# Seven-product matrix sums: the second sum of a unit begun from a copy of the first product, and x normalised by even and odd tokens

## The chip, the core and the metric

The kernel runs on one core of a Trainium2 chip. Each core has a matmul engine (TensorE, PE in the profile, with its weight loads as PEld), VectorE (DVE), ScalarE (ACT), GpSimd (POOL) and SyncE (SP), which run side by side and wait for each other by semaphores. Matrices lie in SBUF, matmul results in PSUM, which has eight banks of 128 x 512 float32. The metric is device time in microseconds of one execution. Before the change it is 1780.31 us, the median of three runs (1779.6 to 1780.34).

## What is computed

A decoder of two layers on 512 tokens of width 1024, all float32. In each layer, cut to what matters here:

```python
x = x + 0.5 * swiglu(rms_norm(x, ffn1_norm[l]), ffn1_w_in[l], ffn1_w_out[l])
h = rms_norm(x, mix_norm[l]) @ w_mix_in[l]
y = concatenate([short_conv_mixer(...), hgrn2_mixer(...), fox_mixer(...)])
x = x + y @ w_mix_out[l]
x = x + 0.5 * swiglu(rms_norm(x, ffn2_norm[l]), ffn2_w_in[l], ffn2_w_out[l])

def swiglu(h, w_in, w_out):
    gate, up = split(h @ w_in, 2)      # w_in is 1024 x 5632, w_out 2816 x 1024
    return (silu(gate) * up) @ w_out
```

The two layers have four of these SwiGLU blocks. The change touches nothing else; the three token mixers stay as they are.

## The kernel before

**Tiling.** x is held transposed in `xT` (128 features x 8 blocks x 512 tokens). A float32 factor is split in a rounded part `hi` (float32r) and the remainder `lo`, and `mm3` (L423) makes each product of blocks from three matmuls: hi x hi (L429), hi x lo (L435), lo x hi (L436). ScalarE makes hi, VectorE makes lo.

**A SwiGLU block.** The 22 blocks of 128 hidden features are taken in pairs. `cover` (L668) does the first 6 (first SwiGLU) or 4 (the others) in the plain way, while the norm of x is found; its table `ENTRY` says at which step the norm, the normalised quarters of x, their splitting and other small work are put in. Then `halved` (L823) does the rest by a scheme of seven products in place of eight for a 2 x 2 block product. A pair of hidden blocks is a unit of the way in, ("I", w): the two halves are of the 1024 features, of gate and up, and of the tokens. The hidden blocks are cut in three chunks (`CHUNKS`); while chunk c + 1 goes in, chunk c goes out to x, in two units ("O", (c, g)), g being one of two column groups. The last chunk goes out plainly (the matmuls with hh).

**The order.** `plan` (L90) writes it out: patterns such as "IIIIO" + "IIO" * 11 + "IOIO" interleave the products of both ways. The first SwiGLU has 84 such products, the others 91, and each is 24 matmuls of 256 columns. Per product n, `plan` also lists smaller work: loads of a 512 x 256 quarter of the weights into one of eight buffers x0 to x7 (SyncE, L854), a transfer that adds a second quarter onto it (GpSimd, L858 and L901), sums of quarters on VectorE (`total`, L871: S2 is the sum S of two quarters, S3 the difference of S and a third), sums of hidden values (L898) and the splitting of hidden values for a way-out product (`moving`, L887). Work that may move is put where `load`, an estimate of VectorE's work per product, is least.

**One product.** The loop that begins at L955 takes product n, then:

- `prepare` (L873) for product n + 3: ScalarE rounds its weights (L883), and after the product's own work VectorE takes the remainder (L885). There are three buffers hl, so this begins when product n has ended;
- for a way-in unit: P1 goes to a bank `a`, and ScalarE copies its negative to SBUF as g1 (L978); P2 has a bank of its own, VectorE takes g1 - P2 (L981), ScalarE the Silu of it (L324). P6 is accumulated on P1 in bank a, and ScalarE copies it to g2 (L985); P5 goes to a third bank and is copied to u2 (L988); P7 goes on in bank a and VectorE adds it to u2 (L991); P3 goes on in P5's bank and is added to g2 (L994), then Silu; after P4, VectorE multiplies out the hidden values (L1008, L1009 in the last chunk, which ScalarE and VectorE then split to hh, L1018 and L1019);
- for a way-out unit: VectorE adds the product, halved and with its sign, to the quarters of x that need it (L973), once for each of the seven.

ScalarE, VectorE, GpSimd and SyncE take this work each in one fixed order (`follow`), so an instruction that waits holds up all behind it on its engine.

**Normalising.** `normalise` (L787) multiplies a quarter of x (four feature blocks x 256 tokens) by gain and inverse norm, in four instructions (L793), stored token after token. `two` (L810) splits a quarter or a sum of quarters (L719) to hi and lo (L816, L817, L821) and reads it by a step of two: all even tokens, then all odd ones, which is how the matmul takes them.

**Banks.** `bank` takes the next of a tag's banks (mm 3, sc 2, pt 2, po 1) from a pool that rotates. A SwiGLU's way in uses one set of four (mm and po, or sc and pt), its way out the other.

Of the kernel before, what the change touches and what calls it, by code (L numbers as in the profile page):

```python
# [8 lines left out]
F32 = mybir.dt.float32  # L9
# [5 lines left out]
ALU = mybir.AluOpType  # L15
# [62 lines left out]


def plan(covered):  # L80

# [21 lines left out]
    def between(a, b, *what):  # L103
# [51 lines left out]
    for c in range(2):  # L155
        n0 = {p: at["O", (c, 0), p] for p in ORDER_OUT}

        last = at["I", CHUNKS[c + 1][0] + (4, 2)[c], "P4"] - 1

        place = {}  # L160
        for i, p in enumerate(ORDER_OUT):
            a = at["O", (c, 1), ORDER_OUT[i - 2]] if i > 1 else n0["P2"] - 3
# [36 lines left out]
class Trunk:  # L199
# [8 lines left out]
    def __init__(self, ctx, tc):  # L208
        self.tc = tc
        self.nc = tc.nc  # L210
        nc = self.nc
        self.uid = 0
        self.ntog = 0
        self.tab, self.tab_users = None, []
# [92 lines left out]

    def bank(self, tag):
        return self.ps.tile([P, T], F32, tag=tag, name=self.n(tag), bufs=BANKS[tag])

# [357 lines left out]
    def cover(self, fp, w_in, w_out, covered, mean, begin):  # L668
# [28 lines left out]
        def squares():  # L697

            norm.append(self.bank("pt" if self.ntog % 2 == 0 else "po"))
            i = self.sum_norm(norm[0])  # L700
            if begin is None:
                self.follow("p", i)
# [84 lines left out]
    def normalise(self, fp, a, b):  # L787

        H = T // 2
        t = fp.tile([P, 4, H], F32, tag=f"r{2 + 2 * a + b}", name=self.n("xn"))  # L790
        for k in range(4):
            i = 4 * a + k
            self.follow("v", self.nc.vector.scalar_tensor_tensor(  # L793
                out=t[:, k, :], in0=self.xT[:, i, b * H : (b + 1) * H],
                scalar=(self.gain if a == b else self.ngain)[:, i : i + 1],
                in1=self.inv[:, b * H : (b + 1) * H], op0=ALU.mult, op1=ALU.mult,
            ))
        self.xn[a, b] = t
# [11 lines left out]
    def two(self, hi, lo, src, other):  # L810

        nc = self.nc
        src = src.rearrange("p k t -> p (k t)").rearrange("p (n h) -> p h n", h=2)
        if other:
# [8 lines left out]
    def halved(self, fp, w_in, w_out, covered, deal):  # L823
# [63 lines left out]
        def moving(c, p):  # L887

            hi, lo = (
                fp.tile([P, 2, T], F32R, tag=f"m{w}", name=self.n("m"), bufs=2) for w in "hl"  # L890
            )
            a, v = self.two(hi, lo, self.quarter(fp, c, *SUM[p]), p in NEGATIVE)
            A(a), V(v)
            mov[c, p] = hi, lo
# [32 lines left out]
        self.hh, self.hl = [], []  # L927
        names = (("mm", "mm", "mm", "po"), ("sc", "sc", "pt", "pt"))

# [13 lines left out]
        ring = {"I": (self.ntog + 1) % 2, "O": self.ntog % 2}  # L943
        used = {"I": 0, "O": 0}
# [10 lines left out]
        for n, (kind, w, p) in enumerate(seq):  # L955
            u = kind, w
            new = ("P1", "P2", "P5")
            k = {"P2": "c", "P5": "b", "P3": "b"}.get(p, "a")
            if p in new:
                work[u, k] = bank(kind)  # L960
            acc = work[u, k]
            product(u, p, acc, p in new, p in ("P2", "P3", "P4"), n in (0, 7))
            rest = prepare(*seq[n + LEAD]) if n + LEAD < len(seq) else None
            if kind == "O":
                c, g = w

                for r, b, f in {
                    "P2": ((0, 0, -0.5),), "P1": ((0, 0, -0.5),), "P5": ((1, 1, -0.5),),
                    "P6": ((0, 1, -0.5),), "P7": ((1, 1, 0.5),), "P3": ((0, 1, 0.5),),
# [6 lines left out]
            elif p == "P1":  # L976
                work[u, "g1"] = g1 = tmp("g1")
                A(nc.scalar.activation(g1, acc, AF.Copy, scale=-1.0))  # L978
            elif p == "P2":
                g1 = work[u, "g1"]  # L980
                V(nc.vector.tensor_sub(g1, g1, acc))  # L981
                A(self.act(g1, g1, AF.Silu))
            elif p == "P6":
# [904 lines left out]
```

## Time and profile before

| | |
|---|---|
| median of the runs | 1780.31 us (1779.6 to 1780.34) |
| the profiled execution | 1781.39 us, its span in the profile 1779.6 us |
| granted TensorE clock | 1.000 |
| PE busy in the span | 1761.0 us, 99% |
| DVE busy | 1439.3 us, 81% |
| ACT busy | 1022.1 us, 57% |
| POOL busy | 176.9 us, 10% |
| seven-product stretches (us from the span's start) | 77.6 to 304.3, 615.6 to 863, 936 to 1183.3, 1494 to 1741.5 |
| mean transfer rate | 147 GB/s |

How to read it: an instruction stands as line, engine, operation, out<-in by the program's names, shape and number. A group's idle time is what its engine sat idle just before its instructions, and the arrow names what ended it. TensorE's matmuls are pipelined: each is shown from its start to a modelled end, which overlaps the next ones, so a busy TensorE says less than the distance between the starts. A lost stretch of TensorE's time is found where two starts lie further apart than usual.

### The profile page before, as it was taken

The numbers are of one execution on the slowest core, as the hardware profiler recorded it, in microseconds if no ns is written. First come the engines' busy times: TensorE is split into PE (matmuls) and PEld (weight loads), VectorE is DVE, ScalarE is ACT, GpSimd is POOL, SyncE is SP. The second block draws the span as 40 slices with busy tenths as digits, with TensorE's granted clock in tenths as the row PEclk, the third lists the DMA queues.
The fourth block names the chain that finished last, engine by engine and source line by source line (L and its number), as shares of the span: only waits on it lengthen the run. The fifth ranks groups of instructions, "written<-read, shape, count | busy, mean of one in ns | idle before, by whom it ended". The sixth has DMA issues, their size and how long they took to land.

```text
span 1779.6 us, 33419 instructions
## 1 busy us (share of the span) xinstructions
PE 1761.0 (99%) x13613; PEld 1644.1 (92%) x13613; DVE 1439.3 (81%) x1991; ACT 1022.1 (57%) x1417; POOL 176.9 (10%) x174
## 2 busy tenths in 40 slices
PE   9999999999999999999999999999999999999999
PEld 7999999888888899999989999998878888999998
DVE  7989888678687888889689897876777779888883
ACT  5555555465666565555456555555656656555652
POOL 0011120100000101112001111201000001020210
PEclk9999999999999999999999999999999999999999
DMA  7659784243543867869276787823434438687762
GB/s 213 189 126 195 182 177 105 75 117 89 134 108 103 237 137 164 194 167 177 83 210 138 172 186 198 168 73 83 119 92 128 122 102 218 167 159 198 157 141 95
DMA packets 257466, 262.35 MB, mean 147 GB/s; under 512 B 25832, under 2 KB 236528, under 8 KB 257312
## 3 DMA queue, kind: packets, MB, share of 16 engines
q1 hardware_dynamic: 201456, 192.02, 36.0%
q0 software_dynamic: 55840, 68.19, 24.0%
q8 instruction: 107, 1.75, 0.4%
q14 instruction: 47, 0.39, 0.1%
q10 hardware_dynamic: 16, 0.00, 0.0%
HBM read 226.15 MB, written 2.17 MB: 128 GB/s over the span
## 4 chain that ended last, share of the span: by engine, by line
PE 81%; DVE 10%; ACT 5%; issue 2%; DMA 2%; SPq 0%; ACTq 0%; DVEq 0%
PE mm L429 11%; PE mm L436 11%; PE mm L435 11%; PE pt L435 5%; PE pt L436 5%; PE pt L429 5%; PE sc L436 5%; PE sc L429 5%; PE sc L435 5%; PE po L429 3%; PE po L435 3%; PE po L436 3%; DVE hl L416 2%; DVE hl L885 2%; ACT hl L413 1%
## 5 line engine op out<-in xcount | busy, mean ns | idle before, releaser
L883 ACT CAST hl<-w 128x1024 fp32r<-128x1024 f32 x322 | 337.3, 1049 | 305.3 <-PE mm L436 71.6
L885 DVE TENSOR_TENSOR hl<-w,hl 128x1024 fp32r<-128x1024 f32 x322 | 393.3, 1223 | 61.2 <-ACT hl L883 61.1
L416 DVE TENSOR_TENSOR hl<-st,hl 128x1024 fp32r<-128x1024 f32 (+3 forms) x152 | 160.1, 1054 | 108.9 <-ACT hl L413 107.9
L413 ACT CAST hl<-st 128x1024 fp32r<-128x1024 f32 (+3 forms) x151 | 137.6, 911 | 162.9 <-PE po L436 77.2
L429 PE MATMUL mm<-xc,hl 128*128 128x256 f32 (+1 forms) x730 | 200.7, 275 | 1.2 <-ACT g L985 0.8
L436 PE MATMUL mm<-xc,hl 128*128 128x256 f32 x728 | 200.4, 275 | 0.6 <-DVE hl L885 0.6
L435 PE MATMUL mm<-xc,hl 128*128 128x256 f32 x728 | 200.3, 275 | 0.0
L429 PE MATMUL sc<-xc,hl 128*128 128x256 f32 (+1 forms) x530 | 145.9, 276 | 2.9 <-ACT g L985 2.3
L436 PE MATMUL sc<-xc,hl 128*128 128x256 f32 x528 | 145.4, 275 | 0.6 <-DVE hl L885 0.6
L435 PE MATMUL sc<-xc,hl 128*128 128x256 f32 x528 | 145.3, 275 | 0.0
L429 PEld LDWEIGHTS mm<-xc,hl 128*128 128x128 f32 x730 | 140.1, 192 | 2.0 <-ACT g L985 0.9
L436 PEld LDWEIGHTS mm<-xc,hl 128*128 128x128 f32 x728 | 139.8, 192 | 0.9 <-DVE hl L885 0.9
L435 PEld LDWEIGHTS mm<-xc,hl 128*128 128x128 f32 x728 | 139.8, 192 | 0.0
L429 PE MATMUL pt<-xc,hl 128*128 128x256 f32 (+1 forms) x482 | 132.1, 275 | 0.0
L435 PE MATMUL pt<-xc,hl 128*128 128x256 f32 x480 | 132.1, 275 | 0.0
L436 PE MATMUL pt<-xc,hl 128*128 128x256 f32 x480 | 132.0, 275 | 0.0
L429 PE MATMUL mm<-x,hl 128*128 128x512 f32 x272 | 105.8, 389 | 0.0
L429 PEld LDWEIGHTS sc<-xc,hl 128*128 128x128 f32 x530 | 101.7, 192 | 4.1 <-ACT g L985 2.7
L435 PE MATMUL mm<-x,hl 128*128 128x512 f32 x272 | 103.1, 379 | 0.0
L436 PE MATMUL mm<-x,hl 128*128 128x512 f32 x272 | 103.1, 379 | 0.0
L436 PEld LDWEIGHTS sc<-xc,hl 128*128 128x128 f32 x528 | 101.4, 192 | 0.9 <-DVE hl L885 0.9
L435 PEld LDWEIGHTS sc<-xc,hl 128*128 128x128 f32 x528 | 101.4, 192 | 0.0
(506 smaller groups left out, 5471.0 us busy)
## 6 DMA issues: line engine op xcount, KB each, us to landing
w<-in_ffn_w_in_dram SPq DMA_DIRECT2D x140, 512.0 KB, 5.9
w<-in_ffn_w_out_dram SPq DMA_DIRECT2D x64, 512.0 KB, 5.2
w<-in_ffn_w_out_dram POOLq DMA_DIRECT2D x56, 512.0 KB, 8.6
w<-in_ffn_w_in_dram POOLq DMA_DIRECT2D x39, 512.0 KB, 8.4
st<-in_w_mix_in_dram SPq DMA_DIRECT2D x72, 256.0 KB, 3.0
st<-in_ffn_w_in_dram SPq DMA_DIRECT2D x70, 256.0 KB, 3.8
w<-S POOLq DMA_DIRECT2D x35, 512.0 KB, 4.8
st<-in_ffn_w_out_dram SPq DMA_DIRECT2D x24, 512.0 KB, 3.6
```

The source lines that it names most:

```text
L413: a = nc.scalar.copy(hi, src[:, c : c + w])
L416: b = nc.vector.tensor_sub(lo, src[:, c : c + w], hi)
L429: i = nc.tensor.matmul(acc[:, c], ah, bh[:, c.start // 2 : c.stop // 2, :], start=first and c.start == 0, stop=False, skip_group_check=True,)
L435: nc.tensor.matmul(acc, ah, bl, start=False, stop=False, skip_group_check=True)
L436: i = nc.tensor.matmul(acc, al, bh, start=False, stop=last, skip_group_check=True)
L883: A(nc.scalar.copy(hi, src))
L885: return lambda: V(nc.vector.tensor_sub(lo, src, hi))
```

## The change

It has four parts.

1. Units for which `seeded` is true (all four way-out units, and the way-in units 10, 12, 14, 18 and 20, between whose P1 and P2 there stands a way-out product): as P1 ends, ScalarE copies its bank into a second bank (`nc.scalar.copy(work[u, "c"], acc)`), and P2 is accumulated there. For a way-in unit the copy of P1 to SBUF and VectorE's g1 - P2 go, and the Silu reads the bank with scale -1. For a way-out unit the x update of P1 goes, and that of P2 stands for both. The other way-in units (4, 6, 8 and 16, or 6, 8 and 16) stay as they were.
2. The way out begins with P1 (`ORDER_OUT`), the patterns are changed so that an O stands between P1 and P2 of the units named, and the estimates in `load` are changed. With them, loads, sums and splittings move to other products and other buffers.
3. `normalise` reads x and the inverse norm by a step of two and stores even tokens and odd tokens apart, and `two` reads the result without a step. The splitting of hidden values (`moving`) reads by a step of two as before.
4. Banks are named one by one: within `halved` each unit's bank is fixed, and elsewhere `turns` counts them.

```diff
-ORDER_OUT = ("P2", "P1", "P5", "P6", "P7", "P3", "P4")
+ORDER_OUT = ("P1", "P2", "P5", "P6", "P7", "P3", "P4")
...
+WAYS = (
+    "IIIIO" + "IIO" * 4 + "IIIO" + "IO" + "IIO" * 5 + "IOIO", "IIIIO" + "IOIIO" * 3 + "IIOIOIO" + "IIO" + "IOIOO",
+)
+def seeded(u):
+    return u[0] == "O" or u[1] >= CHUNKS[1][0] and u[1] not in (f for f, _ in CHUNKS)
...
-    for c, pattern in ((0, "IIIIO" + "IIO" * 11 + "IOIO"), (1, "IIIIO" + "IOIIO" * 5 + "IOIOO")):
+    for c, pattern in enumerate(WAYS):
...
         1024 + (
-            512 if kind == "O" else {"P2": 512, "P7": 512, "P3": 512}.get(p, 0) if p != "P4"
-            else 1024 if w < CHUNKS[2][0] else 2048
+            (576 if p != "P1" else 0) if kind == "O" else
+            576 if p in ("P7", "P3") or p == "P2" and not seeded((kind, w)) else
+            0 if p != "P4" else 704 if w < CHUNKS[2][0] else 2176
         )
...
-    def bank(self, tag):
-        return self.ps.tile([P, T], F32, tag=tag, name=self.n(tag), bufs=BANKS[tag])
+    def bank(self, tag, i=None):
+        if i is None:
+            i = self.turns[tag]
+            self.turns[tag] = (i + 1) % BANKS[tag]
+        return self.ps.tile([P, T], F32, tag=f"{tag}{i}", name=self.n(tag))
...
-        t = fp.tile([P, 4, H], F32, tag=f"r{2 + 2 * a + b}", name=self.n("xn"))
+        t = fp.tile([P, 2, T], F32, tag=f"r{2 + 2 * a + b}", name=self.n("xn"))
...
-                out=t[:, k, :], in0=self.xT[:, i, b * H : (b + 1) * H],
+                out=t[:, :, k * P : (k + 1) * P], in0=unwoven(self.xT[:, i, b * H : (b + 1) * H]),
                 scalar=(self.gain if a == b else self.ngain)[:, i : i + 1],
-                in1=self.inv[:, b * H : (b + 1) * H], op0=ALU.mult, op1=ALU.mult,
+                in1=unwoven(self.inv[:, b * H : (b + 1) * H]), op0=ALU.mult, op1=ALU.mult,
...
-        def bank(kind):
-            used[kind] += 1
-            return self.bank(names[ring[kind]][(used[kind] - 1) % 4])
+        def bank(u, k):
+            kind, w = u
+            at = {"a": 0, "c": 2, "b": 2}[k] + w[1] if kind == "O" else {"a": w % 4, "c": 1, "b": 3}[k]
+            return self.bank(*names[ring[kind]][at])
...
-            new = ("P1", "P2", "P5")
+            new = ("P1", "P5") if seeded(u) else ("P1", "P2", "P5")
...
             product(u, p, acc, p in new, p in ("P2", "P3", "P4"), n in (0, 7))
+            if p == "P1" and seeded(u):
+                work[u, "c"] = bank(u, "c")
+                A(nc.scalar.copy(work[u, "c"], acc))
             rest = prepare(*seq[n + LEAD]) if n + LEAD < len(seq) else None
...
-                    "P2": ((0, 0, -0.5),), "P1": ((0, 0, -0.5),), "P5": ((1, 1, -0.5),),
+                    "P2": ((0, 0, -0.5),), "P1": (), "P5": ((1, 1, -0.5),),
...
             elif p == "P1":
-                work[u, "g1"] = g1 = tmp("g1")
-                A(nc.scalar.activation(g1, acc, AF.Copy, scale=-1.0))
+                if not seeded(u):
+                    work[u, "g1"] = g1 = tmp("g1")
+                    A(nc.scalar.activation(g1, acc, AF.Copy, scale=-1.0))
             elif p == "P2":
-                g1 = work[u, "g1"]
-                V(nc.vector.tensor_sub(g1, g1, acc))
-                A(self.act(g1, g1, AF.Silu))
+                if seeded(u):
+                    work[u, "g1"] = g1 = tmp("g1")
+                    A(self.act(g1, acc, AF.Silu, scale=-1.0))
+                else:
+                    g1 = work[u, "g1"]
+                    V(nc.vector.tensor_sub(g1, g1, acc))
+                    A(self.act(g1, g1, AF.Silu))
```

More of the change, by code (lines that the diff above doesn't have):

```diff
@@ L212, in __init__ @@
         self.uid = 0
+        self.turns = dict.fromkeys(BANKS, 0)
         self.ntog = 0
@@ L697, in squares @@
         def squares():
-            norm.append(self.bank("pt" if self.ntog % 2 == 0 else "po"))
+            norm.append(self.bank("po") if self.ntog % 2 else self.bank("pt", 1))
             i = self.sum_norm(norm[0])
@@ L891, in moving @@
             )
-            a, v = self.two(hi, lo, self.quarter(fp, c, *SUM[p]), p in NEGATIVE)
+            src = self.quarter(fp, c, *SUM[p]).rearrange("p k t -> p (k t)")
+            a, v = self.two(hi, lo, unwoven(src), p in NEGATIVE)
             A(a), V(v)
@@ L956, in halved @@
             u = kind, w
-            new = ("P1", "P2", "P5")
+            new = ("P1", "P5") if seeded(u) else ("P1", "P2", "P5")
             k = {"P2": "c", "P5": "b", "P3": "b"}.get(p, "a")
             if p in new:
-                work[u, k] = bank(kind)
+                work[u, k] = bank(u, k)
             acc = work[u, k]
             product(u, p, acc, p in new, p in ("P2", "P3", "P4"), n in (0, 7))
+            if p == "P1" and seeded(u):
+                work[u, "c"] = bank(u, "c")
+                A(nc.scalar.copy(work[u, "c"], acc))
             rest = prepare(*seq[n + LEAD]) if n + LEAD < len(seq) else None
```

6 lines of the change are left out of this document (2 added, 4 removed).

## The prediction

> **What bounds the kernel now.** I read the page first, then the busy time by stretches, then the order of time on each engine around TensorE's gaps.
>
> ```profile
> PE 1761.0 (99%) x13613; PEld 1644.1 (92%) x13613; DVE 1439.3 (81%) x1991; ACT 1022.1 (57%) x1417; POOL 176.9 (10%) x174
> ```
>
> The ends of matmuls are modelled and overlap the next one, so 99% alone proves little; the pace does. In the order of time, the first matmul of one product and the first of the next:
>
> ```profile
> 201.15 0.28 PE L429 MATMUL pt<-m,hl 128*128 128x256 f32 x1
> ...
> 203.83 0.28 PE L429 MATMUL mm<-xc,hl 128*128 128x256 f32 x1
> ```
>
> A product is 24 matmuls and takes 2.68 us, 0.1117 us each, though each is shown 0.28 long. The four stretches of seven-product work, from the view by stretches (columns: length, then PE busy and its instructions, PEld, DVE, ACT, POOL):
>
> ```profile
> 77.60:304.30 226.70, 226.36 (x2020) 225.77 (x2020) 195.84 (x203) 132.19 (x145) 32.23 (x27) 1.00 0.72 159
> 615.60:863.00 247.40, 245.68 (x2188) 244.74 (x2188) 215.79 (x227) 144.98 (x160) 36.45 (x31) 1.00 0.72 160
> 936.00:1183.30 247.30, 245.91 (x2189) 244.92 (x2188) 215.14 (x227) 144.69 (x160) 35.12 (x30) 1.00 0.71 160
> 1494.00:1741.50 247.50, 245.75 (x2189) 244.76 (x2188) 216.01 (x226) 143.86 (x160) 36.51 (x31) 1.00 0.71 160
> ```
>
> At 0.1117 us a matmul the lengths would be 225.6, 244.4, 244.5 and 244.5. TensorE loses 1.1, 3.0, 2.8 and 3.0 us: 9.9 us is all that a change inside these stretches can win. VectorE is busy 87% of them, so it is the engine that can make TensorE wait. The second stretch shows where (its products counted from 0; these begin products 3, 4, 5, 6 and 79, 80, 81, 82):
>
> ```profile
> 623.79 0.28 PE L429 MATMUL pt<-xc,hl 128*128 128x256 f32 x1
> 627.79 0.38 PE L429 MATMUL sc<-xc,hl 128*128 128x256 f32 x1 [1.16 <-ACT g L985]
> 630.57 0.28 PE L429 MATMUL pt<-xc,hl 128*128 128x256 f32 x1
> 633.64 0.35 PE L429 MATMUL sc<-xc,hl 128*128 128x256 f32 x1 [0.22 <-DVE u L991]
> ...
> 829.46 0.28 PE L429 MATMUL sc<-xc,hl 128*128 128x256 f32 x1
> 832.14 0.28 PE L429 MATMUL mm<-m,hl 128*128 128x256 f32 x1
> 835.19 0.38 PE L429 MATMUL sc<-xc,hl 128*128 128x256 f32 x1
> 838.51 0.28 PE L429 MATMUL mm<-m,hl 128*128 128x256 f32 x1
> ```
>
> Against 2.68, product 3 takes 4.00 (1.32 lost) and product 5 3.07 (0.39): the entry. Product 80 takes 3.05 (0.37 lost) and 81 3.32 (0.64): the tail. Two places hold 2.7 of the 3.0 us. The groups by line say how far the entry stall repeats:
>
> ```profile
> L429 PE MATMUL mm<-xc,hl 128*128 128x256 f32 (+1 forms) x730 | 200.7, 275 | 1.2 <-ACT g L985 0.8 <-DVE u L991 0.3
> L429 PE MATMUL sc<-xc,hl 128*128 128x256 f32 (+1 forms) x530 | 145.9, 276 | 2.9 <-ACT g L985 2.3 <-DVE u L991 0.4
> ```
>
> The way in uses sc and pt in stretches 2 and 4 and mm in 1 and 3: about 1.15 idle each in 2 and 4, 0.8 in 3.
>
> **Part one, the seeded sums.** In five units of the way in and four of the way out per stretch, P2 is accumulated on a copy of P1. For each way-in unit VectorE loses a subtraction (L981), for each way-out unit one x update (L973); ScalarE's copy to SBUF (L978) becomes a copy into PSUM, and the way out gains four such copies.
>
> ```profile
> L973 DVE SCALAR_TENSOR_TENSOR xT<-mm,xT 128x512 f32<-128x512 f32 x42 | 28.8, 686 | 3.1 <-PE mm L436 2.4
> L981 DVE TENSOR_TENSOR g<-g,mm 128x512 f32<-128x512 f32 x13 | 9.0, 694 | 0.1
> L978 ACT ACTIVATE g<-mm 128x512 f32<-128x512 f32 x13 | 7.7, 595 | 0.0
> ```
>
> VectorE gives up 20 x 0.69 + 16 x 0.69 = 25 us, ScalarE takes 16 x 0.6 = 9.5 us; no row has ScalarE writing PSUM, so 0.6 is L978's time, and an eighth either way would not show. Nearly all of the 25 us lies under TensorE's 2.68 us steps and is worth nothing. The new wait is P2's first matmul on the copy. One product stands between, so the copy has 2.68 us; it now stands ahead of the next rounding (L883) in ScalarE's queue and needs 0.6. It is late only where ScalarE is held up as P1 ends, which is in the tail:
>
> ```profile
> 826.70 1.05 ACT L883 CAST hl<-w 128x1024 fp32r<-128x1024 f32 x1 [3.00 <-DMA w<-in_ffn_w_in_dram]
> 828.28 1.07 ACT L1018 CAST hh<-y 128x1024 fp32r<-128x1024 f32 x1 [0.53 <-DVE y L1009]
> 829.24 1.05 ACT L883 CAST hl<-w 128x1024 fp32r<-128x1024 f32 x1
> 829.39 1.23 DVE L1019 TENSOR_TENSOR hh<-y,hh 128x1024 fp32r<-128x1024 f32 x1
> 832.26 1.22 DVE L871 TENSOR_TENSOR S<-w,w 128x1024 f32<-128x1024 f32 x1
> 833.59 1.05 ACT L883 CAST hl<-S 128x1024 fp32r<-128x1024 f32 x1 [3.30 <-DVE S L871]
> ```
>
> Unit 20's P1 moves from product 78 to 77, its P2 stays at 79 (829.46), P6 at 81. ScalarE is held by late weights until 826.70, then by y until 828.28; the copy runs at 829.24 to 829.84: P2 starts 0.4 late. Behind it, the rounding for product 80 ends 830.9 and its remainder on VectorE about 832.1. The sum S then starts at 832.0 instead of 832.26 (an x update now stands behind it, not ahead), its rounding ends 834.4, its remainder 835.6, where product 81, begun at 829.86 + 2 x 2.68 = 835.2, wants it for its third matmul at 835.45: 0.15 late. So 0.55 lost instead of 1.01: a gain of 0.46, 1.8 in four stretches. Bounds: 0 (the copy keeps the whole loss) and 4.0 (the weights land earlier and all goes).
>
> **Part two, x in even and odd order.** The stride of two moves from 28 operand splittings (ScalarE's rounding and VectorE's remainder) to 64 normalisations:
>
> ```profile
> L885 DVE TENSOR_TENSOR hl<-w,hl 128x1024 fp32r<-128x1024 f32 x322 | 393.3, 1223 | 61.2 <-ACT hl L883 61.1
> L821 DVE TENSOR_TENSOR xc<-xn,xc 128x1024 fp32r<-128x1024 f32 x16 | 23.1, 1446 | 4.6 <-ACT xc L821 4.6
> L883 ACT CAST hl<-w 128x1024 fp32r<-128x1024 f32 x322 | 337.3, 1049 | 305.3 <-PE mm L436 71.6 <-PE pt L436 65.7 <-issue 53.1
> L821 ACT CAST xc<-xn 128x1024 fp32r<-128x1024 f32 x16 | 24.7, 1545 | 6.6 <-DVE xn L719 6.2 <-DVE xn L793 0.4
> L1402 DVE TENSOR_TENSOR t<-t,q x4: 411/420/430, 398.2 to 1277.2; 128x256 f32<-128x256 f32 x4
> L1409 DVE TENSOR_TENSOR t<-kb,b 128x256 f32<-128x256 f32 x20 | 8.3, 416 | 0.0
> ```
>
> Contiguous, an operand saves 0.22 on VectorE and up to 0.5 on ScalarE. L1402 reads two SBUF operands by a step of two and takes 0.42, as the contiguous L1409: the added cost of a normalisation is between 0 and 2 x 0.22/4 = 0.11. I take 0.04, near L1402, which has its size and both strided inputs: 16 x 0.04 = 0.6 a stretch. What it is worth is read at the entry, where VectorE has no gap from the first normalisation to the subtraction that product 3's stall hangs on, but one:
>
> ```profile
> 617.77 1.38 DVE L817 SCALAR_TENSOR_TENSOR xc<-xn,xc 128x1024 fp32r<-128x1024 f32 x1 [0.24 <-ACT xc L816]
> 623.89 0.63 ACT L324 ACTIVATE g<-g 128x512 f32<-128x512 f32 x1 [1.49 <-DVE g L981]
> 624.95 1.35 ACT L821 CAST xc<-xn 128x1024 fp32r<-128x1024 f32 x1
> ```
>
> Five remainders ahead save 1.1, the gap 0.24; less 0.6, the subtraction comes 0.7 earlier. Then on ScalarE the operand at 624.95 takes 0.3 less, and the copy of P6 (L985) that frees the bank for product 4 comes 1.0 earlier. Product 5's 0.39 stays, since its queue moves with it. Gain 1.0 in stretches 2 and 4, the whole 0.8 in 3, none in 1: 2.8. Bounds: at 0 extra all of 1.32 and part of 0.39 go (some 4.2 in all); at 0.11 the subtraction is 0.4 later and nothing is won (0.3 lost).
>
> The Trainium skill says otherwise here: its "SBUF — State Buffer", Specifications (TRN2), has 16-byte lines that give full bandwidth at two hits each, so fp32 at a step of two should be free. L1402 agrees; L821's 1545 against 1049 does not, and I go by L821 for the splittings. By the Trainium skill alone this part is worth 0, and the gain below is 2.8 us smaller.
>
> **Part three, order and buffers.** The way out's P1 now goes first, so its quarter of the weights is held six products longer, and loads behind it get buffers later. Two matter, both unit 18's, in each stretch. Its second quarter waits for the buffer of the way out's P2, whose remainder is this DVE row (old order); the ACT row is the rounding that needs it:
>
> ```profile
> 787.86 1.23 DVE L885 TENSOR_TENSOR hl<-w,hl 128x1024 fp32r<-128x1024 f32 x1 [0.39 <-ACT hl L883]
> ```
> ```profile
> 794.87 1.05 ACT L883 CAST hl<-w 128x1024 fp32r<-128x1024 f32 x1 [0.69 <-ACT hh L1018]
> ```
> ```profile
> DMA to landing us min/median/max: 3.5/5.4/12.0
> ```
>
> The row ends at 789.1; VectorE's queue is about 0.6 later there in the new order (a splitting and a sum of the hidden values have come where two x updates left), so the load issues at 789.7 and lands at 793.2, 795.1 or 801.7. Queued behind that rounding on ScalarE are unit 18's copy and its sum's rounding; behind its remainder on VectorE, the sum S and the difference that follows it, which itself waits for the last quarter, loaded one remainder later. Product 68 starts at 829.46 - 11 x 2.68 = 799.98, 69 at 802.66. Landing up to 796.5 is hidden; 797.5 costs 0.75 through S; I take 0.3 a stretch: 1.2. Bounds 0 and, at 12.0, about 4.8 a stretch. Elsewhere, in stretches 2 and 4, the first bank after the stretch is no longer an idle one; an exposed x update is 0.69, I take 0.2 each: 0.4. The banks of the mixer stages are renamed only.
>
> **Sum:** -1.8 - 2.8 + 1.2 + 0.4 = -3.0 on the profiled span of 1779.6, so 1776.6. The median of the runs, 1780.31, stands 0.7 over the span: 1777.3.
>
> **Rivals.** (a) *The stride costs nothing on either side*: L821's extra comes from the work beside it, and the entry stall stays. For: L1402. Against: all 28 splittings are long. Without the 2.8: 1780.1, no change. The Trainium skill's page named above would have this. (b) *Slower: the loads of unit 18 hold ScalarE.* From a landing over 6.8 us after issue (796.5) on, every late us goes into two in-order queues. At 9 us (798.7): rounding to 799.8, remainder 801.1, product 68 loses 0.9; S 802.2, its rounding 803.3, remainder 804.5 where product 69 wants 803.8: 0.7 more. 1.65 x 4 = 6.6 instead of 1.2: 1782.7; if the last quarter is late as well, 1785. For: accumulating transfers share the engines there. Against: the median of 5.4. (c) *All stalls go*: the lighter VectorE queue clears entry and tail and loads come early: 1780.3 - 9 = 1771.
>
> **How the numbers follow.** Forecast 0.43 (its own range 1774.5 to 1779.5, part of it beyond 0.2%), (a) 0.20, (b) 0.24, (c) 0.13. 0.2% is 3.6 us, about what a measurement of this kernel can tell from no change. Faster by more: all of (c), and 0.25 of the forecast's 0.43: 0.38. Slower: (b) and a little, 0.24. Within: 0.38. Range 1772.5 to 1783.5: it leaves half of (c) and a third of (b) out.
>
> **What would show it.** Operand rows of xc at 1.05 (ScalarE) and 1.22 (VectorE), normalisations at 0.48 to 0.59; product 3 of stretches 2 to 4 at 3.0 instead of 4.0; P2 of unit 20 waiting on ScalarE's copy for about 0.4; no L973 of P1; VectorE busy some 25 us less. A wait of ScalarE on a transfer before product 68, or of VectorE before unit 18's difference, speaks for (b). I am wrong if TensorE loses more than 9.9 us in the four stretches together.

## The result, and the profile after

The changed kernel takes 1782.44 us (median of 19 runs, 1780.59 to 1787.9) against 1780.18 us before (19 runs, 1779.04 to 1781.57): a ratio of 1.0015, 95% interval 1.0008 to 1.0022. By the ratio it is slower by 2.7 us where 3.0 faster was forecast. Its runs spread over 7 us, those before over 2.5. The profiled execution took 1782.51 us, its span 1780.7 (before 1781.39 and 1779.6).

The changed kernel's lines stand lower: its matmul lines L444, L450 and L451 are L429, L435 and L436 of before, L897 and L899 are L883 and L885, L885 is L871 (the sums of quarters), L835 is L821, L808 is L793, L734 is L719, L868, L872 and L916 are L854, L858 and L901, L1005 is L981, L1009 is L985, L1033 is L1009, L1042 is L1018, and its L981 is the seed copy. First the busy times on the page, then the four stretches in the view by stretches (length, then PE, PEld, DVE, ACT, POOL busy, clock, DMA share and GB/s; the share adds up the packets' own times over 16 engines, so it can pass 1):

```profile
PE 1759.3 (99%) x13613; PEld 1642.1 (92%) x13613; DVE 1415.1 (79%) x1955; ACT 1015.0 (57%) x1433; POOL 176.9 (10%) x174
```
```profile
77.35:304.20 226.85, 226.44 (x2020) 225.86 (x2019) 189.14 (x194) 133.78 (x149) 32.22 (x27) 1.00 0.72 160
615.55:863.85 248.30, 245.88 (x2188) 244.78 (x2187) 210.03 (x219) 145.22 (x164) 36.62 (x31) 1.00 0.71 159
937.25:1185.45 248.20, 245.76 (x2188) 244.70 (x2187) 208.06 (x217) 144.50 (x163) 34.83 (x30) 1.00 0.71 159
1495.40:1742.45 247.05, 245.34 (x2188) 244.62 (x2188) 210.33 (x217) 144.31 (x163) 36.62 (x31) 1.00 0.71 160
```

VectorE lost 24 us, about the 25 it was to lose. Against 0.1117 us a matmul, TensorE now loses 1.2, 3.9, 3.8 and 2.6 us, 11.5 in place of 9.9: by the prediction's own test, it is wrong. Three places of the second stretch show where. (A fourth, product 37, loses 0.5 in this stretch alone; no run was aimed at it.) Its entry (products 3 to 6) and tail (77, 78, 79, 80 and 81) in the order of time on TensorE:

```profile
623.72 0.28 PE L444 MATMUL pt<-xc,hl 128*128 128x256 f32 x1
627.41 0.38 PE L444 MATMUL sc<-xc,hl 128*128 128x256 f32 x1 [0.85 <-ACT g L1009]
630.19 0.28 PE L444 MATMUL pt<-xc,hl 128*128 128x256 f32 x1
633.13 0.35 PE L444 MATMUL sc<-xc,hl 128*128 128x256 f32 x1
```
```profile
824.39 0.28 PE L444 MATMUL sc<-xc,hl 128*128 128x256 f32 x1
827.07 0.28 PE L444 MATMUL mm<-m,hl 128*128 128x256 f32 x1
831.22 0.38 PE L444 MATMUL sc<-xc,hl 128*128 128x256 f32 x1 [1.22 <-ACT sc L981]
834.00 0.28 PE L444 MATMUL mm<-m,hl 128*128 128x256 f32 x1
836.68 0.28 PE L444 MATMUL sc<-xc,hl 128*128 128x256 f32 x1
```

Product 3 takes 3.69 (4.00 before), product 5 2.94 (3.07). In the tail product 80 is clean, but 78 stretches to 4.15: unit 20's P2, product 79, waits for its seed copy (L981), and 1.47 is lost. In the four stretches 0.54, 1.47, 1.75 and 0.98 are lost here; 0.36 of the 1.75 goes inside product 78, ahead of the copy. The third place is new: unit 14's P2 (46, or 39 in the first stretch), at 741.04 here, loses 0.08, 0.27, 0.85 and 0.10.

**The tail on ScalarE.** Its instructions ahead of the copy, and the issue of unit 20's first, second and last quarter on SP's queue, merged in one row that begins with the first:

```profile
821.25 1.05 ACT L897 CAST hl<-w 128x1024 fp32r<-128x1024 f32 x1 [3.60 <-DMA w<-in_ffn_w_in_dram]
...
829.64 1.05 ACT L1042 CAST hh<-y 128x1024 fp32r<-128x1024 f32 x1 [2.89 <-DVE y L1033]
830.59 0.58 ACT L981 COPY sc<-sc 128x512 f32<-128x512 f32 x1
```
```profile
810.84 8.88 SPq L868 DMA_DIRECT2D w<-in_ffn_w_in_dram  x3
```

Unit 20's first quarter is issued at 810.84 and its rounding can begin only at 821.25. Before, the same load is issued at 812.07, and P1's rounding at 822.67 doesn't wait for it. The crowd is not new: in 810 to 820 and 820 to 830 us the DMA share is 1.17 and 1.18 before, 1.20 and 1.19 after. But with P1 one product earlier the rounding is needed 2.7 us earlier and the load is issued only 1.2 us earlier, so ScalarE stands still 3.6 us for it. The work behind it in the queue (Silu, `moving`) is late, so VectorE's y is late, so the rounding of the hidden values is late, and the copy stands behind that: 830.59, where the prediction had 829.24.

**Unit 14: GpSimd's queue.** Its transfers that add to a buffer, before and then after (start, time of the issue, and the idle time ahead with what ended it):

```profile
707.63 1.29 POOL L858 DMA_DIRECT2D w<-in_ffn_w_out_dram  x1 [6.89 <-DVE w L871]
711.37 0.89 POOL L901 DMA_DIRECT2D w<-S  x1 [2.45 <-DVE S L871]
712.83 1.30 POOL L858 DMA_DIRECT2D w<-in_ffn_w_out_dram  x1 [0.58 <-DVE hl L885]
720.13 1.28 POOL L858 DMA_DIRECT2D w<-in_ffn_w_out_dram  x1 [6.00 <-DVE hl L885]
722.22 1.28 POOL L858 DMA_DIRECT2D w<-in_ffn_w_in_dram  x1 [0.81 <-DMA w<-in_ffn_w_in_dram]
```
```profile
715.13 0.89 POOL L916 DMA_DIRECT2D w<-S  x1 [14.96 <-DVE S L885]
715.68 2.97 POOL L872 DMA_DIRECT2D w<-in_ffn_w_out_dram  x2
721.58 1.28 POOL L872 DMA_DIRECT2D w<-in_ffn_w_out_dram  x1 [2.93 <-DVE hl L899]
727.43 1.28 POOL L872 DMA_DIRECT2D w<-in_ffn_w_in_dram  x1 [4.57 <-DMA w<-in_ffn_w_in_dram]
```

The planner puts unit 12's sum S a product later (33, not 32; in the first stretch 26, not 25). The new order of products does this, not the new costs in `load`: with either set of costs `plan` gives 33 in the new order and 32 in the old. The transfer that adds S (L916) stays at 33, while P5 of the way out's second unit goes from 33 to 34 and takes a transfer with it. So L916 now stands ahead of two transfers of the way out that before went one ahead and one behind. GpSimd waits 15 us for S, then issues all three at once. The DMA share (last column but one) before, in 710 to 720, and after in that and the next two stretches of 10 us:

```profile
710.00:720.00 10.00, 10.00 (x92) 10.00 (x91) 9.54 (x10) 5.76 (x8) 2.19 (x2) 1.00 1.04 182
```
```profile
710.00:720.00 10.00, 9.74 (x87) 9.55 (x87) 9.41 (x10) 5.00 (x7) 3.52 (x3) 1.00 0.36 59
720.00:730.00 10.00, 10.00 (x92) 10.00 (x92) 9.12 (x9) 6.22 (x7) 2.57 (x2) 1.00 1.17 232
730.00:740.00 10.00, 10.00 (x92) 10.00 (x91) 7.10 (x9) 5.01 (x6) 0.00 (x0) 1.00 1.14 282
```

The DMA engines idle, then crowd. SP issues the quarter that unit 14's sum S begins with at 717.83 before and at 718.15 after, 0.3 us apart, so a late buffer is not the cause. But it lands late, and GpSimd can issue the transfer that adds to it only at 727.43 instead of 722.22. VectorE's sum S of unit 14 waits for that transfer (before, it starts at 735.45 without a wait), and the remainder of P2's weights, which P2's third matmul needs, stands two rows behind it in VectorE's queue. That remainder before, then the sum and the remainder after:

```profile
737.78 1.22 DVE L885 TENSOR_TENSOR hl<-w,hl 128x1024 fp32r<-128x1024 f32 x1
```
```profile
737.81 1.23 DVE L885 TENSOR_TENSOR S<-w,w 128x1024 f32<-128x1024 f32 x1 [1.30 <-DMA w<-in_ffn_w_in_dram]
740.15 1.22 DVE L899 TENSOR_TENSOR hl<-w,hl 128x1024 fp32r<-128x1024 f32 x1
```

P2 begins at 741.04, and its remainder is ready only at 741.37.

### The profile page after: what moved, and what is told of

The parts are those of the page before. It is cut to its first block, busy times and chain, and to the rows that moved or that the text cites. A ratio compares the mean times of both kernels' runs of the same rounds, so it can differ in the third digit from the quotient of the medians.

```text
span 1780.7 us, 33364 instructions
## 1 busy us (share of the span) xinstructions
PE 1759.3 (99%) x13613; PEld 1642.1 (92%) x13613; DVE 1415.1 (79%) x1955; ACT 1015.0 (57%) x1433; POOL 176.9 (10%) x174
## 3 DMA queue, kind: packets, MB, share of 16 engines
q8 instruction: 107, 1.75, 0.4%
## 4 chain that ended last, share of the span: by engine, by line
PE 82%; DVE 8%; ACT 5%; DMA 3%; issue 2%; SPq 0%; ACTq 0%; DVEq 0%
PE mm L444 12%; PE mm L451 11%; PE mm L450 11%; PE sc L444 6%; PE sc L451 6%; PE pt L451 5%; PE pt L444 5%; PE sc L450 5%; PE pt L450 5%; PE po L444 3%; PE po L450 3%; PE po L451 3%; DVE hl L431 2%; DMA w<-in_ffn_w_in_dram 2%; ACT hl L428 1%
## 5 line engine op out<-in xcount | busy, mean ns | idle before, releaser
L897 ACT CAST hl<-w 128x1024 fp32r<-128x1024 f32 x322 | 338.1, 1050 | 297.2 <-PE pt L451 66.9
L899 DVE TENSOR_TENSOR hl<-w,hl 128x1024 fp32r<-128x1024 f32 x322 | 391.8, 1221 | 95.3 <-ACT hl L897 94.6
L444 PE MATMUL mm<-xc,hl 128*128 128x256 f32 (+1 forms) x684 | 187.6, 275 | 2.1 <-ACT mm L981 1.6
L451 PE MATMUL mm<-xc,hl 128*128 128x256 f32 x680 | 187.5, 276 | 0.6 <-DVE hl L899 0.6
L450 PE MATMUL mm<-xc,hl 128*128 128x256 f32 x680 | 187.2, 275 | 0.0
L444 PE MATMUL pt<-xc,hl 128*128 128x256 f32 x546 | 149.7, 275 | 0.0
L450 PE MATMUL pt<-xc,hl 128*128 128x256 f32 x544 | 149.7, 275 | 0.0
L451 PE MATMUL pt<-xc,hl 128*128 128x256 f32 x544 | 149.6, 275 | 0.0
L444 PEld LDWEIGHTS mm<-xc,hl 128*128 128x128 f32 x684 | 131.1, 192 | 3.0 <-ACT mm L981 2.0
L444 PE MATMUL sc<-xc,hl 128*128 128x256 f32 (+1 forms) x466 | 128.3, 276 | 3.9 <-ACT sc L981 2.0
L451 PEld LDWEIGHTS mm<-xc,hl 128*128 128x128 f32 x680 | 130.5, 192 | 1.1 <-DVE hl L899 0.8
L450 PEld LDWEIGHTS mm<-xc,hl 128*128 128x128 f32 x680 | 130.5, 192 | 0.0
L451 PE MATMUL sc<-xc,hl 128*128 128x256 f32 x464 | 128.1, 276 | 0.3 <-DVE hl L899 0.3
L450 PE MATMUL sc<-xc,hl 128*128 128x256 f32 x464 | 127.7, 275 | 0.0
L444 PE MATMUL mm<-x,hl 128*128 128x512 f32 x272 | 105.8, 389 | 0.0
L444 PEld LDWEIGHTS pt<-xc,hl 128*128 128x128 f32 x546 | 104.7, 192 | 0.0
L450 PEld LDWEIGHTS pt<-xc,hl 128*128 128x128 f32 x544 | 104.4, 192 | 0.0
L451 PEld LDWEIGHTS pt<-xc,hl 128*128 128x128 f32 x544 | 104.4, 192 | 0.0
L450 PE MATMUL mm<-x,hl 128*128 128x512 f32 x272 | 103.1, 379 | 0.0
L451 PE MATMUL mm<-x,hl 128*128 128x512 f32 x272 | 103.1, 379 | 0.0
```

What stands on the lines that cost most here:

```text
L444: i = nc.tensor.matmul(acc[:, c], ah, bh[:, c.start // 2 : c.stop // 2, :], start=first and c.start == 0, stop=False, skip_group_check=True,)
L450: nc.tensor.matmul(acc, ah, bl, start=False, stop=False, skip_group_check=True)
L451: i = nc.tensor.matmul(acc, al, bh, start=False, stop=last, skip_group_check=True)
L897: A(nc.scalar.copy(hi, src))
L899: return lambda: V(nc.vector.tensor_sub(lo, src, hi))
```

## The experiments

Each kernel ran beside the kernel before. Its median comes first, then its ratio to that kernel, with the 95% interval. "The wait at unit 14" is that of its P2. Waits are those of the one profiled run of each kernel, read as above.

**The parts apart.** x in even and odd order alone: before plus the diff's lines in `normalise`, `two` and `moving`.

> The kernel before with the even and odd order of the normalised x alone, and nothing of the seeds, the order or the buffers. If the entry gains what the changed kernel's trace shows (products 3 and 5 of stretches 2 to 4 together 0.44, 0.51 and 0.52 us shorter): 1780.2 - 1.5 = 1778.7 us. The prediction's own term was -2.8 (1777.4). If the entry's gain in the changed kernel came from elsewhere (buffers, banks): 1780.2.

1779.48 us, 0.9992 (0.9983 to 1.0001). Products 3 and 5 of the second stretch begin at:

```profile
623.41 0.28 PE L429 MATMUL pt<-xc,hl 128*128 128x256 f32 x1
626.99 0.38 PE L429 MATMUL sc<-xc,hl 128*128 128x256 f32 x1 [0.73 <-ACT g L985]
629.77 0.28 PE L429 MATMUL pt<-xc,hl 128*128 128x256 f32 x1
632.71 0.35 PE L429 MATMUL sc<-xc,hl 128*128 128x256 f32 x1
```

They take 3.58 and 2.94 (3.69 and 2.94 in the changed kernel). The ratio is worth -1.4 us, half of the prediction's 2.8, and its interval just takes in no change; the trace bears it out, with products 3 and 5 of stretches 2 to 4 together 0.5 shorter in each. All but that:

> The changed kernel with the old normalisation and the old strided operand splittings: seeds, order and buffers alone. If the two parts add: 1782.4 + 1.5 = 1783.9 us. If the lighter splittings of the way out's moving quarters also feed the stalls of the tail (ScalarE ahead of its late weights is given nothing by them): 1782.4 to 1783.

1784.49 us, 1.0027 (1.0018 to 1.0036): 2.1 over the changed kernel by the ratios. The parts add, within the intervals. So seeds, order and buffers together cost 4.8 us, where the prediction's terms for them add up to -0.2.

The order without copies, first with the planner's costs as changed, then with the costs of a kernel without seeds. The first edit, cut (`started` takes the place of `seeded` wherever a product is made, and `plan` keeps `seeded`):

```diff
+        started = lambda u: False
...
-            new = ("P1", "P5") if seeded(u) else ("P1", "P2", "P5")
+            new = ("P1", "P5") if started(u) else ("P1", "P2", "P5")
```

> The changed kernel in its own order of products, loads and buffers, but no second sum is seeded: each unit's P2 starts its own bank, with the subtraction on VectorE (way in) and the x update of P1 (way out) back. Theory Q: no product waits for a copy, so the waits ahead of unit 20's second product (4.7 us over four stretches) and most of those ahead of unit 14's (1.2 us) go, the tail's waits on the sum S return with about 0.8 a stretch: 1782.4 - 5.9 + 3.2 = 1779.7 us (1778.5 to 1781). Rival W: the copies are not the cause, the order and the late weights are: 1782 to 1783.5.

1788.13 us, 1.0045 (1.0032 to 1.0057): far above both theories. The second, beside the first:

```diff
 def seeded(u):
 
-    return u[0] == "O" or u[1] >= CHUNKS[1][0] and u[1] not in (f for f, _ in CHUNKS)
+    return False
...
-            (576 if p != "P1" else 0) if kind == "O" else
+            576 if kind == "O" else
```

> The changed order of products, buffers and loads with the even and odd order of x, but no seeds, and the planner's costs set as for a kernel without seeds (the kernel with no copies kept the costs of one with them). The prediction's third part priced order and buffers at 1.6 us, with -2.8 for x: 1779. Theory O (order and buffers are what costs, and the seeds only win part of it back): near the kernel with no copies, less what the planner can mend: 1785 to 1788.5 us, with waits at unit 14's second product and at products 78 to 81 of each stretch. If the earlier kernel's loss came from the planner's wrong costs: 1780 to 1782.

1790.32 us, 1.0053 (1.0040 to 1.0065). ScalarE's longest waits in 815 to 835 us, in the second stretch, summed by cause (us in all, times, longest):

```profile
ACT hl L897 <- DMA w<-in_ffn_w_in_dram: 5.8, 2, 5.0
ACT hh L1044 <- DVE y L1035: 2.8, 1, 2.8
```

Without any copy the late weights hold ScalarE for 5.0 us, unit 14 waits 1.15, 0.81, 1.58 and 1.23, and products 77 to 82 (70 to 75 in the first stretch) lose 2.0 to 3.0 a stretch (before 1.2). Without seeds, order and buffers cost 9.4 + 1.4 = 10.8 us (this ratio less that of x alone, times 1780), and the seeds win back 6.7 (to the changed kernel's 2.7). With the kernel above, which keeps the changed kernel's plan, the two are 9.4 and 5.3.

The seeds in the old order, for the three units where it allows them:

```diff
+            early = u in (("I", 10), ("I", 14), ("I", 18))
+            new = ("P1", "P5") if early else ("P1", "P2", "P5")
...
+            if p == "P1" and early:
+                work[u, "c"] = bank(kind)
+                A(nc.scalar.copy(work[u, "c"], acc))
```

> The kernel before in its own order and with its own loads, with the second sum of units 10, 14 and 18 begun as ScalarE's copy: the three units of the way in where the old order already has a product of the way out between P1 and P2. The prediction's step (a seed whose VectorE work is covered is worth nothing, and its copy costs nothing away from the tail): 1780.5, within 0.7. If taking work off VectorE is worth something by itself (6.2 us of subtractions): 1779.5 or below; if a copy holds TensorE even in the old order: 1781.5 or above, with waits at products 25, 46 and 68.

1782.24 us, 1.0005 (0.9996 to 1.0013): no difference can be told. The median lies where a copy that holds TensorE was to put it, but products 25, 46 and 68 have no wait. So a copy holds nothing up there, and the 6 us taken off VectorE bring nothing that shows.

**The tail.** The rounding of unit 18's hidden values one product later, so that the copy is ahead of it:

```diff
+            if held is not None:
+                hh, y, hl = held
+                A(nc.scalar.copy(hh, y))
+                V(nc.vector.tensor_sub(hl, y, hh))
+                held = None
...
+                if w == 18:
+                    held = hh, y, hl
+                else:
```

> The changed kernel, with unit 18's rounding of the hidden values (L1042 in the changed kernel) and its remainder issued one product later, behind the seed copy of unit 20 instead of ahead of it. Theory Q (the copy is late because it stands in ScalarE's queue behind this rounding, which waits for VectorE's y): the wait of unit 20's second product goes from 0.54, 1.47, 1.75 and 0.98 us in the four stretches to under 0.1 each, and some 0.3 a stretch comes back where the sum S is next late: 1782.4 - 4.7 + 1.2 = 1779 us (1778 to 1780). Rival W (weights that land late in the new buffer order set the end of the tail, whatever stands in the queue): the wait moves to the next products and the time stays within 0.7 us of the changed kernel's, 1782.

1780.32 us, 0.9998 (0.9990 to 1.0007). The copy in the second stretch, and the start of unit 20's P2:

```profile
828.50 0.57 ACT L981 COPY sc<-sc 128x512 f32<-128x512 f32 x1 [1.09 <-PE sc L451]
```
```profile
830.98 0.28 PE L444 MATMUL sc<-xc,hl 128*128 128x256 f32 x1
```

The copy waits for its product alone and is done 1.9 us early, and the wait for it is gone. The time misses the expectation by a microsecond. The profiled run, the slowest of its eleven (1782.64), shows two places where it may lie. Unit 14's waits are 0.8, 1.3, 1.2 and 0.2. And products 78, 79 and 81 now lose 0.5, 0.7, 1.6 and 0.5 a stretch together (74 in the first): about half of the copy's wait moved on to them, as rival W had it. Unit 20 alone unseeded (P2 in its own bank, L1005 back):

> The changed kernel with unit 20 alone unseeded, its order, loads and all other seeds as changed. Theory Q (the copy is the cause): the 4.7 us ahead of unit 20's second product go, the subtraction and what it holds cost 0.3 a stretch: 1779 us (1778 to 1780.2). Theory L (the weights are the cause, and without the copy the stall stands at the next operand, as in the kernel with no copies at all, where products 78, 79 and 81 lost 2.2, 2.3 and 2.0 us in stretches 2 to 4): 1782 to 1785.

1781.27 us, 1.0004 (0.9995 to 1.0013), between the two: P2 starts on time, but matmuls within products 78, 79 and 81 wait 1.0 to 1.8 together in stretches 2 and 3 (2.3 and 2.1 in the kernel without copies). The old order in the second half:

```diff
-    "IIIIO" + "IIO" * 4 + "IIIO" + "IO" + "IIO" * 5 + "IOIO", "IIIIO" + "IOIIO" * 3 + "IIOIOIO" + "IIO" + "IOIOO",
+    "IIIIO" + "IIO" * 4 + "IIIO" + "IO" + "IIO" * 5 + "IOIO", "IIIIO" + "IOIIO" * 5 + "IOIOO",
...
-    return u[0] == "O" or u[1] >= CHUNKS[1][0] and u[1] not in (f for f, _ in CHUNKS)
+    return u[0] == "O" or u[1] >= CHUNKS[1][0] and u[1] not in (f for f, _ in CHUNKS) and u[1] != 20
```

> The changed kernel with the old order of products in the second half of each stretch (unit 20's P1 at product 78, its P2 behind it, unseeded), the rest as changed. Theory Q: no wait for the copy (4.7 us over four stretches and 1.2 of the products behind it), the old tail's 1.0 a stretch instead: 1782.2 - 5.9 + 4.1 = 1780.4 us (1779.5 to 1781.5). Rival W (the late weights of unit 20 in the new order of loads set the tail anyway): 1782 or above.

1786.21 us, 1.0029 (1.0020 to 1.0039): Q's expectation failed. With the old order of the second half but the new buffers, products 78 to 82 lose 2.1 in the second stretch, where before loses 1.2 with the same products. Unit 20's first quarter is not needed earlier here. ScalarE waits 3.4 us for a transfer of the way out in its place, until 821.63 (before 1.7, until 819.05), though GpSimd issues it at 809.19 (before 808.97). So the copy's wait is only one place where late weights come out, and unit 20's quarter is not the only late one. Why this transfer lands later is open. Taking one transfer out of the crowd:

```diff
-            when(split["P5"] + 3, 5, "add", u, 0, 2)
+            when(split["P5"] + (6 if w == (1, 1) else 3), 5, "add", u, 0, 2)
```

> The changed kernel with one accumulating transfer taken out of the crowd ahead of the tail: the one that the way out's product P7 (82) needs is issued three products later, behind unit 20's. Theory L (unit 20's first quarter, issued at 810.84 in the second stretch and landed only at 821.2 with the DMA engines at a share of 1.2, holds ScalarE for 3.6 us and makes y, the rounding of the hidden values and the copy late): the quarter lands 1.5 to 2.5 us earlier, ScalarE's wait ahead of it falls to under 2.5, the wait for the copy (0.54, 1.47, 1.75, 0.98) falls by a half or more, and the time by 2 to 3: 1780 us (1779 to 1781.5). Theory Q alone (the copy's place behind the rounding, whatever lands): the wait stays over 1 us a stretch and the time at 1782.4.

1781.83 us, 1.0005 (0.9996 to 1.0014). The copy's waits halve in all (0.43, 1.08, 0.43 and 0.43), but ScalarE's wait is still 3.2 in the second stretch, and the time doesn't show a gain beyond the interval. Unit 14 cost this profiled run 3.3.

**Unit 14.** The suspected fault put into the kernel before:

```diff
-                between(m - 1, m, "total", u, "S2")
-                when(max(m, split["P2"]), 6, "adds", u)
+                between(m - (w != 12), m, "total", u, "S2")
+                when(max(m, split["P2"]), 4.5 if w == 12 else 6, "adds", u)
```

> The kernel before, with unit 12's sum S put one product later and the accumulation that waits for it ahead of the way out's ready one, as the changed kernel has it; nothing else of the change. Theory H: unit 14's second product (46) waits 0.3 to 1.3 us in stretches 2 to 4 and something in the first, which it doesn't do before, and the time is 1.3 to 4 us above before: 1782.5 us (1781.5 to 1784.3). Rival B: no wait there, 1780.3.

1783.91 us, 1.0017 (1.0008 to 1.0026). GpSimd's queue and the shares of 710 to 730:

```profile
714.24 0.89 POOL L901 DMA_DIRECT2D w<-S  x1 [13.75 <-DVE S L871]
714.78 2.97 POOL L858 DMA_DIRECT2D w<-in_ffn_w_out_dram  x2
721.28 1.28 POOL L858 DMA_DIRECT2D w<-in_ffn_w_out_dram  x1 [3.52 <-DVE hl L885]
727.28 1.28 POOL L858 DMA_DIRECT2D w<-in_ffn_w_in_dram  x1 [4.71 <-DMA w<-in_ffn_w_in_dram]
```
```profile
710.00:720.00 10.00, 10.00 (x92) 10.00 (x91) 8.78 (x10) 5.65 (x7) 3.52 (x3) 1.00 0.46 73
720.00:730.00 10.00, 10.00 (x92) 10.00 (x91) 9.14 (x10) 6.00 (x7) 2.57 (x2) 1.00 1.18 247
```

Both pictures are the changed kernel's, and unit 14's P2 waits 0.62, 0.41, 1.49 and 0.72, 3.2 us in all, beside 3.0 above before by the ratio. The mend in the changed kernel:

```diff
-                when(max(m, split["P2"]), 6, "adds", u)
+                when(max(m, split["P2"]) + (w == 12), 6, "adds", u)
```

> The changed kernel with one accumulating transfer of each stretch moved in GpSimd's queue: the one that adds unit 12's sum to its second quarter is issued one product later, behind the two accumulations of the way out that stand ready. Theory H (that transfer waits for the sum S of unit 12, which the planner put a product later, and holds the two ready ones; the DMA engines idle at a share of 0.36 for 10 us and then all transfers crowd at 1.15, so unit 14's weights land late and its second product, 39 or 46 of the stretch, starts late): the share in 710 to 720 us rises towards the 1.04 of before, the wait at unit 14 (0.1 to 0.9 a stretch in the changed kernel, up to 1.3 in the one with the later rounding) falls under 0.2, and the time by 1.3 to 3.4: 1780.2 us (1779 to 1781.5). Rival B (unit 14's weights are late because their buffers are freed late, whatever GpSimd issues): the wait stays and the time with it, 1782.2.

1782.48 us, 1.0009 (1.0000 to 1.0017). In the profiled run, its fastest (1780.08), the DMA share of 710 to 720 us is 0.85, and unit 14's P2 no longer waits (in the third stretch 0.5 moves to products 42 and 43). The issue times above speak against rival B. But the median doesn't move, so by the time alone this run decides nothing. With the later rounding:

> Both repairs of the changed kernel: the later rounding of unit 18's hidden values and the later accumulation of unit 12. The kernel with the first alone stood at 1780.3 and lost 3.4 us at unit 14 in its profile. Theory H: 1780.3 - 2.5 = 1777.8 us (1776.9 to 1779.2), faster than before. Rival B: 1780.3.

1778.79 us, 0.9989 (0.9980 to 0.9998): as theory H had it.

**All three, and controls.**

> The later rounding, the later accumulation of unit 12 and the later accumulation for product 82 together. Theory L: the kernel with the first two stood at 1778.8 and still lost 1.4 us ahead of products 79 and 80 in stretches 2 and 3; half of that and some of product 81's 0.45 goes: 1777.3 us (1776 to 1778.5). If the late weights are no cause: 1778.8.

1776.71 us, 0.9976 (0.9967 to 0.9986): faster than both kernels. The stretches of the profiled run, its fastest (1775.00):

```profile
76.05:301.85 225.80, 225.78 (x2020) 225.59 (x2019) 189.06 (x194) 133.72 (x149) 32.21 (x27) 1.00 0.72 160
613.20:859.65 246.45, 245.32 (x2188) 244.56 (x2188) 209.98 (x218) 145.62 (x164) 36.59 (x31) 1.00 0.72 161
933.05:1179.35 246.30, 245.46 (x2188) 244.63 (x2187) 208.87 (x217) 145.36 (x164) 35.63 (x30) 1.00 0.72 160
1489.20:1734.95 245.75, 244.98 (x2188) 244.47 (x2187) 210.08 (x217) 144.26 (x163) 36.60 (x31) 1.00 0.72 161
```

TensorE loses 0.2, 2.1, 1.9 and 1.3, 5.5 in all where before loses 9.9. Without unit 12's mend:

> The three-repair kernel without the repair of unit 12's accumulation. Theory H (that accumulation, held by the sum S ahead of two ready ones, makes unit 14's weights late): the wait at product 46 (39 in the first stretch) is back with 0.1 to 1.3 us a stretch and the time is 1.3 to 3.4 above 1776.7: 1778 to 1780 us. Rival B: 1776.7.

1779.21 us, 0.9989 (0.9981 to 0.9998): 2.3 us above by the ratios, whose intervals overlap a little, with waits at unit 14 of 1.5, 1.2, 1.1 and 0. The tail's mends and x without seeds, in the old order:

> The kernel before with the even and odd order of x and the same two repairs of the tail (unit 18's rounding a product later, the accumulation for product 82 three products later), without seeds and in the old order. If the three-repair kernel's 1776.7 owes its gain to the repairs alone: 1777 us or below. If seeds and order bring something once their transfers are mended: 1778.5 to 1779.5, with the old tail's 0.4 and 0.6 us ahead of products 80 to 82 still there.

1778.63 us, 0.9989 (0.9980 to 0.9998): the old tail stays (products 80 to 82 lose 0.3, 0.6 and 0.2), and seeds and order, once mended, are worth some 2 us more (0.9976 against 0.9989, intervals that overlap a little). No run has the mended order without seeds, so what each of the two brings there is open.

## Why the prediction was wrong

**Part three (order and buffers, +1.6) is the step that failed.** It measured +10.8 without the seeds, nearly all of it at two places: unit 14 (4.8 us of waits) and the tail (10.3, where before has 4.8). How that and the seeds' -6.7 share the 4.8 us that both cost together depends on which is taken out first; that their sum is 4.8 and not -0.2 doesn't. "Two matter, both unit 18's" was the wrong pair: in stretches 2 to 4 products 66 to 71 wait nowhere, in the changed kernel or in the one without copies. Unit 18's load came later, as worked out, and was harmless: it was issued at 789.88 (789.7 forecast) and landed 4.4 us later. The two that matter are unit 12's sum, which changed its place in the planner and held GpSimd's queue, and unit 20's first quarter, needed a product earlier while the share stands at 1.2, as it did before. The prediction followed the loads on SP's queue through their buffers and never laid GpSimd's queue of before beside that of after, though the order of both was known. The first is shown from both sides (put into before: +3.0; taken out of the otherwise mended kernel: -2.3). For the second, the late weights are shown in ScalarE's waits, and that the copy is not their cause by the kernels without it. Why transfers land later there, in the old order of the second half too, was only argued and stays open. The 0.4 for the first bank after a stretch shows nowhere: outside the stretches the changed kernel's profile is 0.4 us shorter, and nothing there was tried.

**Part one (seeds, -1.8) was wrong by size, too.** The copy takes 0.57, close to the 0.6 assumed. Taking 25 us off VectorE was to be worth nothing outside the tail. In the old order nothing spoke against it, with three seeds. In the new one the seeds saved 5.3 to 6.7, most of it at unit 14, whose waits add up to 5.7 with the changed plan and no copies and to 1.3 with them. Presumably each operation less counts there because VectorE is already late; no run separates that. In the tail P2 was to start 0.4 late, and 1.47 was lost in the second stretch. That step failed at its start: the copy's 829.24 took over before's times of ScalarE, with weights at 826.70 that hold only the last rounding. The changed order meets its late weights at 821.25, ahead of y.

**Part two (x, -2.8) had the right mechanism and half the size,** -1.4. Groups of after, splittings and normalisations:

```profile
L835 ACT CAST xc<-xn 128x1024 fp32r<-128x1024 f32 x16 | 16.7, 1044 | 9.3 <-DVE xn L734 7.1 <-DVE xn L808 2.2
L835 DVE TENSOR_TENSOR xc<-xn,xc 128x1024 fp32r<-128x1024 f32 x16 | 19.5, 1219 | 3.1 <-ACT xc L835 3.1
L808 DVE SCALAR_TENSOR_TENSOR xn<-xT,ngain,inv 128x256 f32<-128x256 f32 x32 | 16.3, 588 | 0.0
L808 DVE SCALAR_TENSOR_TENSOR xn<-xT,gain,inv 128x256 f32<-128x256 f32 x32 | 16.1, 564 | 0.1
```

The splittings fell as forecast, 1545 to 1044 ns and 1446 to 1219. A normalisation rose from 478 to 576, by 0.10 and not 0.04: close to the upper bound of 0.11, where the lower one was preferred since L1402 was nearest in shape. In the changed kernel this eats VectorE's whole gain ahead of the entry: the subtraction comes 7.55 us after the stretch's first matmul, 7.54 before. (With 16 x 0.10 = 1.6 in place of 0.6, the prediction's own sum would put it 0.26 later, so the gain was counted somewhat too low.) The 0.31 that product 3 wins is ScalarE's one shorter splitting, 1.35 to 1.03.

The Trainium skill, "SBUF — State Buffer", Specifications (TRN2), says that two hits on each 16-byte line give full bandwidth, and that each cross to a new line pays a penalty, whose size it leaves out. Taken to mean that fp32 at a step of two is free, as in the prediction, it agrees neither with the splittings nor with L808.

**Rivals.** (b), the slower side, named the mechanism, late weights that hold ScalarE's queue, in the wrong place. That its 1782.7 lies beside the measured 1782.44 is chance: unit 18, from which it was worked out, cost nothing. (a) falls by the splittings (1545 to 1044 ns) and by L808, (c) by the stalls that stayed. The terms were wrong by 9.2, 4.9 and 1.4 us, the second the other way from the other two, so the sum missed by only 5.7 and the time fell within the stated range. That was luck: the direction was wrong, and the working didn't hold.

## What to carry to other kernels

When the order of work changes, list every engine's queue of before and after side by side, the queue that issues accumulating transfers too, and look for an instruction that waits for a later producer ahead of ones that are ready: it idles the DMA engines first and crowds them afterwards. Price a moved operand by when its data lands in the new order, not by the old timeline shifted. A change that loses may hold a gain behind such a fault: with three pieces of work moved, this one was 0.24% faster than before (0.14 to 0.33%).

## What the runs showed of the hardware

Transfers of one size landed later where they crowd. Time from issue to landing in 715 to 742 us of the changed kernel (queue, number, size, median us):

```profile
w<-in_ffn_w_in_dram SPq DMA_DIRECT2D x5, 512.0 KB, 11.6
w<-in_ffn_w_out_dram POOLq DMA_DIRECT2D x3, 512.0 KB, 11.8
```

GpSimd's accumulating transfers (L858) took 5.5 us at the least and 8.4 in the median over the whole kernel before. Of the five loads on SP's queue the profile tells the landing of one, the quarter for unit 14's P2, issued at 724.85. The same load took 8.8 us before (issued at 724.80) and 5.7 with unit 12's accumulation moved (724.68). The DMA share of 720 to 730 us alone doesn't put the three in order (1.17, 0.90 and 1.12), so how transfers share the engines is not shown.

An accumulating transfer whose data isn't ready holds the ready ones behind it in GpSimd's queue: 15 us here, with the DMA share down to 0.36 and then up to 1.17.

The same step of two costs nothing in one operation (L1402, 420 ns against L1409's 418 in the median), 0.10 of 0.48 us in another (L808), and adds half to ScalarE's rounding (1044 to 1545 ns).

Why the changed kernel's runs spread over 7 us is not shown: the order alone, which waits longer for its weights, spread over 1.2 in its five runs.
